# All eight heads in each recurrence step, and a written order for the conv's products between the steps

## The chip, the cores and the metric

The kernel runs on one core of a Trainium2 chip. The metric is the device time of one execution in microseconds (us); lower is better. An execution counts from its start to its end, and the span of the profile is the part of it that the profiler's records cover.

The engines are named as in the profile: PE is TensorE (matrix products), DVE is VectorE, ACT is ScalarE, POOL is GpSimd, SP is SyncE, which only issues transfers here. Each engine works through its own queue; engines wait for one another by semaphores.

## What is computed

The reference is a model of two layers over a sequence of T = 512 positions with D = 1024 channels, batch 1. Layer 0 mixes with a conv branch and an RWKV-7 branch, layer 1 with windowed attention; each is followed by a gated feed-forward block. The change touches layer 0's mixer, cut here to what matters:

```python
def conv_rwkv_mixer(x, ...):
    p = rms_norm(x, norm_g) @ w_in
    c = p[..., :2 * CONV_W] + conv_in_b                       # CONV_W = 512
    c = c[..., :CONV_W] * jax.nn.sigmoid(c[..., CONV_W:])     # the gated inputs ("glu")
    c = causal_dwconv(c, conv_dw_w, conv_dw_b)                # 31 taps, each channel by itself
    c = jax.nn.silu(layer_norm(c, conv_ln_g, conv_ln_b, CONV_LN_EPS))
    ...                                                       # r, decay, k, v, a, b of 8 heads of 64
    y = rwkv7_recurrence(rh, hs(decay), kh, vh, -kk, kk * hs(a))
    ...                                                       # group norm, bonus term, gate
    return jnp.concatenate([c, y], axis=-1) @ w_out

def step(s, inp):                                             # one position of the recurrence
    r_t, w_t, k_t, v_t, a_t, b_t = inp
    sa = jnp.einsum('bhij,bhj->bhi', s, a_t)
    s = s * w_t[:, :, None, :] + sa[..., None] * b_t[:, :, None, :] + v_t[..., None] * k_t[:, :, None, :]
    return s, jnp.einsum('bhij,bhj->bhi', s, r_t)
```

## The kernel before

Channels lie on the 128 partitions and positions along the free axis, so a tensor of 512 channels is four tiles of 128x512. Matrix products with a 1024-wide weight are made of three parts (high half by high half, and twice a high half by a low half): L150 casts a weight to its high half `whi` on ACT, L151 subtracts to get its low half `wlo` on DVE, and L174 is the product. L183 and L184 do the same to an activation.

**The recurrence** works in chunks of L = 64 positions: NCH = 8 chunks one after another, 8 heads in each. Ahead of it stands the inversion of small triangular systems; its last part are products of 32x32 tiles, L520 and L527, in two halves `g` of two groups of 32 products, whose results ACT copies to `tg` (L522) and `mbt` (L529). A chunk is worked in two half-steps `g` of four heads. Each half-step has five groups of products on TensorE:

- px, L543: operators times the stacked tile `sv` (rows 0 to 63 the state of the chunk, rows 64 to 127 the values), copied to `xs` (L545, on DVE for the first half, on ACT for the second);
- py, L549: the output's first part;
- pu, L556, which needs `xs`; ACT copies it over the old state (L558);
- pS, L562, the new state, which needs that copy. DVE puts it into `sv` of the next chunk: for chunk 0 as a copy (L566), later with the decayed old state `ds` (L553) added (L568);
- py's second part, L570; ACT copies py to `y` (L572).

The px of the next chunk reads the state that L566 or L568 wrote.

**The conv branch**: `glu(j)` makes one block of 128 channels of gated inputs (two products with the weight, L464 to L468, a sigmoid on ACT). Blocks 1 to 3 go through DRAM (`cpad`), come back shifted in four phases as `st` (loads L628, issued by POOL), and are convolved on TensorE, L633: 32 products per block, in groups of four that fill the four column strips, with the weights spread on diagonals `dg` (L623, DVE). L635 on ACT takes a finished block to `accs[j]`. Block 0 has its 31 taps on DVE: L618 on ACT starts the accumulator and 30 instructions of L620 add a tap each. `accs` of the four blocks go through a LayerNorm: sums over blocks L641 to L643, the split L183/L184, a product with ones L647, L652 takes the mean off, L653 squares, the same sums again (`lv`), a reciprocal root, L659 and a SiLU, and the split into `mc`. The group norm of the recurrence's output (L595 to L612) runs in two halves of the sequence and gives `mr`. The output projection takes all of `mc` first, then all of `mr`.

**What sets the order.** A scheduler (the Tile framework) orders the instructions of each engine from the code as written and from its own costs; it sets the conv's products between the recurrence's groups. In the code, the recurrence comes first, then the gated inputs, then the conv; a `table` call marks where ACT switches its function table, and work of that table is tied to it. `banks` and `psum` hand out TensorE's output banks in turn.

Of the kernel before, what the change touches and what calls it, by code (L numbers as in the profile page):

```python
# [19 lines left out]
P = 128  # L20
T = 512
# [7 lines left out]
CST = 540  # L29
# [39 lines left out]
class Net:  # L69
# [186 lines left out]
    def mixer(self):  # L256
# [7 lines left out]
        with ExitStack() as es:  # L264
# [234 lines left out]
            for fc in range(4):  # L499
                values(fc)  # L500

            zp = cst.tile([P, CK - 1], F32, name="zp")
            G.memset(zp, 0.0)
            for j in range(CC):
# [2 lines left out]
            m32 = cst.tile([P, 1, 1, 32], F32, name="m32")  # L507
            for s in range(4):
                G.tensor_copy(m32[s * 32 : s * 32 + 32, 0, 0, :], self.ident[s * 32 : s * 32 + 32, s * 32 : s * 32 + 32])
            mbu = mbt.rearrange("p f e c t -> p (f e c) t")  # L510
            svu = sv.rearrange("p f e c t -> p (f e c) t")
            for d in (1, 0):
# [18 lines left out]


            ys = [el([P, 2, 2, T // 2], "y") for _ in range(2)]
            half = lambda p0: self.psum()[p0 : p0 + 64, 0:256].rearrange("p (h i) -> p h i", h=4)
            heads = [(h, h // 2, h % 2) for h in range(4)]
            for c in range(NCH):
                for g in range(2):
                    mt = mts[g]
                    fs = slice(2 * g, 2 * g + 2)
                    st = sv[0:64, fs, :, c, :]  # L540
                    px = half(64)
                    for h, f, e in heads:
                        nc.tensor.matmul(px[:, h, :], lhsT=mt[:, f, e, c, 0:L], rhs=sv[:, 2 * g + f, e, c, :], start=True, stop=True)  # L543
                    xs = tr.tile([P, 4, L], F32, tag="xs", name="xs", bufs=2)[64:128]
                    (S.copy if g else V.tensor_copy)(xs, px)  # L545

                    py = self.psum()[:, 0 : 2 * L].rearrange("p (f t) -> p f t", f=2)
                    for h, f, e in heads:
                        nc.tensor.matmul(py[e * 64 : e * 64 + 64, f, :], lhsT=sv[:, 2 * g + f, e, c, :], rhs=mt[:, f, e, c, L:P],  # L549
                                         start=f == 0, stop=False)  # L550
                    if 0 < c < NCH - 1:
                        ds_ = tr.tile([64, 2, 2, L], F32, tag="xs", name="ds", bufs=2)
                        V.tensor_tensor(out=ds_, in0=st, in1=dl[:, fs, :, c : c + 1].to_broadcast([64, 2, 2, L]), op=ALU.mult)  # L553
                    pu = half(0)
                    for h, f, e in heads:
                        nc.tensor.matmul(pu[:, h, :], lhsT=mbt[64:128, 2 * g + f, e, c, :], rhs=xs[:, h, :], start=True, stop=True)  # L556

                    S.copy(st, pu.rearrange("p (f e) i -> p f e i", f=2))  # L558
                    if c < NCH - 1:
                        pS = half(0)  # L560
                        for h, f, e in heads:
                            nc.tensor.matmul(pS[:, h, :], lhsT=bkt[:, 2 * g + f, e, c, :], rhs=sv[:, 2 * g + f, e, c, :], start=True, stop=True)  # L562
                        pS4 = pS.rearrange("p (f e) i -> p f e i", f=2)
                        so = sv[0:64, fs, :, c + 1, :]
                        if c == 0:
                            V.tensor_copy(so, pS4)  # L566
                        else:
                            V.tensor_tensor(out=so, in0=pS4, in1=ds_, op=ALU.add)  # L568
                    for h, f, e in heads:
                        nc.tensor.matmul(py[e * 64 : e * 64 + 64, f, :], lhsT=sv[0:64, 2 * g + f, e, c, :],  # L570
                                         rhs=mbt[0:64, 2 * g + f, e, c, :], start=False, stop=f == 1)
                    S.copy(ys[g][:, 2 * c // NCH, :, c % 4 * L : (c % 4 + 1) * L], py)  # L572

            self.table("sigmoid_and_others")
            cp0 = ta("glu0")
            for j in range(CC):
                glu(j)
            self.table("natural_log_exp_and_others")


            g2 = ta("g2")
# [31 lines left out]
                    self.split(mr[:, 0, fs, ts], mr[:, 1, fs, ts], y)  # L613


            lt = self.act.tile([P, 2, CC, T], F32, tag="xgl", name="lt")
            accs, sqs = [[lt[:, o, j, :] for j in range(CC)] for o in range(2)]
# [3 lines left out]
            for j in range(1, CC):  # L621
                dg = tr.tile([P, 4, 8, 32], F32, tag="ep", name="dg", bufs=2)
                V.tensor_tensor(out=dg, in0=self.pcs("conv_dw", P)[:, 32 * j : 32 * j + 32].rearrange("p (q g o) -> p q g o", q=4, o=1).to_broadcast([P, 4, 8, 32]), in1=m32.to_broadcast([P, 4, 8, 32]), op=ALU.mult)  # L623
                stk = []
                for q in (2 * j, 2 * j + 1):
                    st = tr.tile([P, 2, CST], F32, tag="t4", name="st", bufs=T4)
                    for s in range(4):
                        G.dma_start(st[s * 32 : s * 32 + 32], cpad[q * 64 : q * 64 + 64, s : s + CST].rearrange("(b p) t -> p b t", p=32))  # L628
                    stk += [st[:, 0], st[:, 1]]
                pc = self.pmm()  # L630
                for g in range(8):
                    for b in range(4):
                        nc.tensor.matmul(pc[b * 32 : b * 32 + 32, :], lhsT=dg[:, b, g, :], rhs=stk[b][:, 4 * g : 4 * g + T],  # L633
                                         start=g == 0, stop=g == 7, tile_position=(0, b * 32))
                S.activation(out=accs[j], in_=pc, func=AF.Identity, bias=self.pc("conv_dw_b", j))  # L635


            def total(zs, name):
# [406 lines left out]
```

## Time and profile before

| | us |
|---|---|
| device time, median of three runs | 1218.25 |
| lowest and highest of the three | 1217.0 and 1220.24 |
| the profiled execution, its own time | 1216.95 |
| span of its profile | 1215.2 |
| PE busy in the span | 1194.8 (98%) |
| DVE busy | 723.4 (60%) |
| ACT busy | 554.3 (46%) |
| POOL busy | 72.0 (6%) |
| mean granted clock of PE | 0.996 |

The share of busy time is a mean over a kernel whose stages differ: the two feed-forward blocks are long rows of products, layer 0's mixer a dependent chain of small ones. A shape such as `128*64 128x64` in a row is what a product reads of its weights and what it streams; an fp32 product has two records in the trace. The time before an instruction stands in brackets with what ended it.

### The profile page before, as it was taken

How to read it: one execution, taken by the hardware profiler on the slowest of the kernel's cores; microseconds unless marked ns; L12 is line 12 of the kernel's file. 1: busy time of each engine (PE TensorE's matmuls, PEld its weight loads, DVE VectorE, ACT ScalarE, POOL GpSimd, SP SyncE). 2: the span in 40 equal slices, each digit the busy share in tenths (PEclk: the TensorE clock that was granted, in tenths of full speed). 3: DMA queues.
4: the chain of work that ended last, by engine and by line, in shares of the span. 5: the costliest groups of instructions: out<-in, count | busy, mean ns of one | idle time of the engine just before them, and what ended most of it. 6: DMA issues, size and time to landing. Idle time of an engine off the chain costs nothing.

```text
span 1215.2 us, 16956 instructions
## 1 busy us (share of the span) xinstructions
PE 1194.8 (98%) x6419; PEld 940.5 (77%) x6419; DVE 723.4 (60%) x1366; ACT 554.3 (46%) x1035; POOL 72.0 (6%) x209
## 2 busy tenths in 40 slices
PE   6999999999999999999999999999999999999998
PEld 5777866568788888888888866668888888888886
DVE  6787866477766555553333778875555555553332
ACT  6878332374534444342222567764543343442221
POOL 4101031000100000000000031100000000000000
PEclk9999998999999999999999999999999999999999
DMA  6144291023322223233333231112222223233331
GB/s 191 37 130 113 96 221 38 2 88 103 97 92 104 94 97 104 87 104 96 96 96 95 87 95 57 41 36 90 101 90 101 103 89 104 88 103 112 113 113 61
DMA packets 65088, 114.43 MB, mean 94 GB/s; under 512 B 15680, under 2 KB 17936, under 8 KB 65008
## 3 DMA queue, kind: packets, MB, share of 16 engines
q1 hardware_dynamic: 60048, 102.25, 26.3%
q0 software_dynamic: 4816, 10.89, 3.5%
q8 instruction: 50, 0.82, 0.3%
q14 instruction: 30, 0.25, 0.1%
q10 hardware_dynamic: 144, 0.23, 0.1%
HBM read 105.40 MB, written 4.26 MB: 90 GB/s over the span
## 4 chain that ended last, share of the span: by engine, by line
PE 94%; DVE 2%; ACT 2%; DMA 1%; issue 1%; SPq 0%; DVEq 0%
PE mm L174 68%; PE bank L174 11%; PE mm L633 2%; PE bank L931 2%; PE bank L957 1%; PE bank L950 1%; PE ps L411 1%; PE ps L543 1%; DMA xT<-in_xT_dram 1%; PE ps L562 1%; PE ps L556 1%; PE ps L570 0%; PE bank L359 0%; PE ps L549 0%; PE ps L520 0%
## 5 line engine op out<-in xcount | busy, mean ns | idle before, releaser
L151 DVE TENSOR_TENSOR wlo<-wraw,whi 128x512 fp32r<-128x512 f32 x364 | 250.8, 690 | 348.0 <-ACT whi L150 347.4
L150 ACT CAST whi<-wraw 128x512 fp32r<-128x512 f32 x364 | 224.9, 619 | 421.3 <-PE mm L174 378.4
L174 PE MATMUL mm<-xgh,whi 128*128 128x512 f32 x896 | 350.9, 392 | 9.8 <-ACT whi L150 8.3
L174 PE MATMUL mm<-xgh,wlo 128*128 128x512 f32 x896 | 351.0, 392 | 0.2 <-DVE wlo L151 0.2
L174 PE MATMUL mm<-xgl,whi 128*128 128x512 f32 x896 | 350.5, 391 | 0.0
L174 PEld LDWEIGHTS mm<-xgh,whi 128*128 128x128 f32 x896 | 168.6, 188 | 47.0 <-ACT whi L150 10.1
L174 PEld LDWEIGHTS mm<-xgh,wlo 128*128 128x128 f32 x896 | 168.5, 188 | 38.7 <-issue 2.4
L174 PEld LDWEIGHTS mm<-xgl,whi 128*128 128x128 f32 x896 | 168.7, 188 | 35.8 <-issue 1.2
L174 PE MATMUL mm<-hh,whi 128*128 128x512 f32 x352 | 136.9, 389 | 0.0
L174 PE MATMUL mm<-hl,whi 128*128 128x512 f32 x352 | 136.9, 389 | 0.0
L174 PE MATMUL mm<-hh,wlo 128*128 128x512 f32 x352 | 136.9, 389 | 0.0
L174 PEld LDWEIGHTS mm<-hh,wlo 128*128 128x128 f32 x352 | 66.1, 188 | 13.8
L174 PEld LDWEIGHTS mm<-hh,whi 128*128 128x128 f32 x352 | 66.1, 188 | 13.8
L174 PEld LDWEIGHTS mm<-hl,whi 128*128 128x128 f32 x352 | 66.1, 188 | 13.5
L720 DVE SCALAR_TENSOR_TENSOR t<-gp,col,t 128x512 f32<-128x512 f32 x88 | 63.5, 745 | 0.0
L717 ACT ACTIVATE t<-gp,col 128x512 f32<-128x512 f32 x44 | 35.7, 816 | 35.3 <-DVE gp L715 34.7
L183 ACT CAST hh<-t 128x512 fp32r<-128x512 f32 x44 | 27.2, 622 | 36.8 <-DVE t L723 36.5
L715 DVE TENSOR_TENSOR gp<-mm,rstd 128x512 f32<-128x512 f32 x44 | 30.3, 692 | 17.3 <-PE mm L174 17.2
L723 DVE TENSOR_TENSOR t<-t,mm 128x512 f32<-128x512 f32 x44 | 30.1, 687 | 17.0 <-PE mm L174 17.0
L101 ACT ACTIVATE t<-t 128x512 f32<-128x512 f32 x44 | 27.7, 630 | 20.4 <-DVE t L720 20.3
L714 POOL MEMSET gp<- 128x2 f32 x44 | 4.5, 104 | 507.7 <-DVE t L720 451.0
L936 DVE CUSTOM_DVE_ANT_0 pr<-bank,mask,nsnk 128x256 f32<-128x256 f32 (+1 forms) x64 | 31.4, 503 | 1.9 <-PE bank L931 1.9
(328 smaller groups left out, 1433.6 us busy)
## 6 DMA issues: line engine op xcount, KB each, us to landing
wraw<-in_w_up_dram SPq DMA_DIRECT2D x88, 512.0 KB, 3.5
wraw<-in_w_down_dram SPq DMA_DIRECT2D x40, 512.0 KB, 3.5
wraw<-in_w_in_dram SPq DMA_DIRECT2D x22, 512.0 KB, 3.6
wraw<-in_w_qkv_dram SPq DMA_DIRECT2D x12, 512.0 KB, 3.5
wraw<-in_w_out_dram SPq DMA_DIRECT2D x8, 512.0 KB, 3.5
wraw<-in_w_o_dram SPq DMA_DIRECT2D x8, 512.0 KB, 3.5
st<-cpad POOLq DMA_DIRECT2D x24, 135.0 KB, 4.4
xT<-in_xT_dram SPq DMA_DIRECT2D x4, 512.0 KB, 8.2
```

Source lines behind the costliest of these rows:

```text
L101: ins = self.nc.scalar.activation(**kw)
L150: nc.scalar.copy(hi, src)
L151: nc.vector.tensor_tensor(out=lo, in0=src, in1=hi.bitcast(F32), op=ALU.subtract)
L174: mm = lambda a, b, **kw: self.nc.tensor.matmul(ps, lhsT=a[:, i, k, :], rhs=b[:, kk, :], **kw)
L183: nc.scalar.copy(hi, src)
L633: nc.tensor.matmul(pc[b * 32 : b * 32 + 32, :], lhsT=dg[:, b, g, :], rhs=stk[b][:, 4 * g : 4 * g + T], start=g == 0, stop=g == 7, tile_pos ...
L715: V.tensor_tensor(out=gp[:, 2:], in0=pg[i], in1=rstd, op=ALU.mult)
L717: S.activation(out=t, in_=gp[:, 2:], func=AF.Identity, scale=self.pc("ffn_conv_w", (3 * l + 2) * FC + f), bias=self.pc("ffn_conv_b", l * F ...
L720: V.scalar_tensor_tensor(out=t, in0=gp[:, j : j + T], scalar=self.pc("ffn_conv_w", (3 * l + j) * FC + f), in1=t, op0=ALU.mult, op1=ALU.add)
L723: V.tensor_tensor(out=t, in0=t, in1=pu[i], op=ALU.mult)
L931: nc.tensor.matmul(pscs[e][:, hp, :nk], lhsT=qr[hs, h // 2, bs], rhs=kd[m][hs, k0 : k0 + nk], start=True, stop=True)
L936: V.tensor_tensor_reduce(out=pr_[:, i, :nk], in0=pscs[e][:, hp, :nk], in1=mask[:, 2 * P - nk :], op0=ALU.add, op1=ALU.min, scale=rq[:, b, ...
```

## The change

1. **Gated inputs.** The loop over `glu(j)` with its table switches moves from behind the recurrence to ahead of the triangles' products, in the order 1, 2, 3, 0.
2. **Conv products in a written order.** The loads, `dg` and the products of a block are issued by a generator, `conv_steps`, four products at a time. `cover(8)` sets the 32 products of block 1 ahead of the triangles' products; then each chunk calls it behind py, behind pu, and for chunks 0 to 3 behind py's second part. The generator is used up with the second burst of chunk 5. Within `tc.manual_schedule(engines={nc.tensor.engine})`, chunks 0 to 5 keep TensorE's instructions in the order of the code. The orders of DVE, ACT and POOL stay the scheduler's.
3. **Eight heads in a step.** Each chunk is one step; groups are of eight products, and copies are 512 wide. `xs` is copied by ACT alone. py takes one whole bank of ring "n".

Line numbers move: L543 px is L587 in the kernel after, L545 is L589, L549 L593, L553 L598, L556 L601, L558 L603, L562 L608, L566 and L568 L612 and L614, L570 L616, L572 L620; L520 is L566, L522 L568, L527 L573, L529 L575; L620 is L666, L623 L524, L633 L539, L635 L542, L641 to L643 L672 to L674, L595 L643, L600 L648, L609 L657, L647 L678, L652 L683.

```diff
@@ ahead of the triangles' products
+            self.table("sigmoid_and_others")
+            cp0 = ta("glu0")
+
+            for j in (1, 2, 3, 0):
+                glu(j)
+            self.table("natural_log_exp_and_others")
...
+            def conv_steps():
+                for j in range(1, CC):
+                    dg, stk = cv[j]
+                    pc = self.pmm()
+                    for g in range(8):
+                        for b in range(4):
+                            nc.tensor.matmul(pc[b * 32 : b * 32 + 32, :], lhsT=dg[:, b, g, :], rhs=stk[b][:, 4 * g : 4 * g + T],
+                                             start=g == 0, stop=g == 7, tile_position=(0, b * 32))
+                        if g == 7:
+                            S.activation(out=accs[j], in_=pc, func=AF.Identity, bias=self.pc("conv_dw_b", j))
+                            if j + 2 < CC:
+                                conv_load(j + 2)
+                        yield
+
+            conv_load(1)
+            conv_load(2)
+            steps = conv_steps()
+
+            def cover(n):
+                for _ in range(n):
+                    next(steps, None)
+
+            cover(8)
@@ the recurrence
-            heads = [(h, h // 2, h % 2) for h in range(4)]
-            for c in range(NCH):
+            heads = [(h, h // 2, h % 2) for h in range(8)]
+            eight = lambda p0: self.psum()[p0 : p0 + 64].rearrange("p (h i) -> p h i", h=8)
+
+            def chunk(c, cover):
...
+                px = eight(64)
+                for h, f, e in heads:
+                    nc.tensor.matmul(px[:, h, :], lhsT=mts[f // 2][:, f % 2, e, c, 0:L], rhs=sv[:, f, e, c, :], start=True, stop=True)
+                xs = td_("xs")[64:128].rearrange("p (h i) -> p h i", h=8)
+                S.copy(xs, px)
+
+                py = self.bank("n")[:, 0 : 4 * L].rearrange("p (f t) -> p f t", f=4)
...
+                cover(1)
+                if 0 < c < NCH - 1:
+                    ds_ = tb_("ds")[0:64].rearrange("p (f e i) -> p f e i", f=4, e=2)
+                    V.tensor_tensor(out=ds_, in0=st, in1=dl[:, :, :, c : c + 1].to_broadcast([64, 4, 2, L]), op=ALU.mult)
+                pu = eight(0)
...
+                S.copy(st, pu.rearrange("p (f e) i -> p f e i", f=4))
+                cover(1)
+                if c < NCH - 1:
+                    pS = eight(0)
...
+                    so = sv[0:64, :, :, c + 1, :]
+                    if c == 0:
+                        V.tensor_copy(so, pS4)
+                    else:
+                        V.tensor_tensor(out=so, in0=pS4, in1=ds_, op=ALU.add)
...
+                cover(c < 4)
                 for g in range(2):
...
+                    S.copy(ys[g][:, 2 * c // NCH, :, c % 4 * L : (c % 4 + 1) * L], py[:, 2 * g : 2 * g + 2, :])
+
+            with tc.manual_schedule(engines={nc.tensor.engine}):
+                for c in range(NCH - 2):
+                    chunk(c, cover)
+            for c in range(NCH - 2, NCH):
+                chunk(c, cover)
```

What this does to the order of the instructions is shown at three places.

TensorE in the kernel before, from the last weight products of the gated inputs through the triangles to the first half-steps (`st,dg` are the conv's products, `tg,sv` and `mbt,tg` the triangles', `sv,mt` px, `mt,sv` py, `xs,mbt` pu, `sv,bkt` pS):

```order
L633 MATMUL mm<-st,dg 32x512 x29
L520 MATMUL ps<-tg,sv 32x32 x32
L633 MATMUL mm<-st,dg 32x512 x4
L527 MATMUL ps<-mbt,tg 32x32 x32
L633 MATMUL mm<-st,dg 32x512
L520 MATMUL ps<-tg,sv 32x32 x32
L527 MATMUL ps<-mbt,tg 32x32 x32
L543 MATMUL ps<-sv,mt 64x64 x4
L549 MATMUL ps<-mt,sv 64x64 x4
L556 MATMUL ps<-xs,mbt 64x64 x4
L633 MATMUL mm<-st,dg 32x512 x3
L562 MATMUL ps<-sv,bkt 64x64 x4
```

The same place on TensorE in the kernel after, through step 0:

```order
L539 MATMUL mm<-st,dg 32x512 x32
L566 MATMUL ps<-tg,sv 32x32 x32
L573 MATMUL ps<-mbt,tg 32x32 x32
L566 MATMUL ps<-tg,sv 32x32 x32
L573 MATMUL ps<-mbt,tg 32x32 x32
L587 MATMUL ps<-sv,mt 64x64 x8
L593 MATMUL bank<-mt,sv 64x64 x8
L539 MATMUL mm<-st,dg 32x512 x4
L601 MATMUL ps<-xs,mbt 64x64 x8
L539 MATMUL mm<-st,dg 32x512 x4
L608 MATMUL ps<-sv,bkt 64x64 x8
L616 MATMUL bank<-mbt,sv 64x64 x8
```

The triangles' four groups now stand in one run behind all of block 1's conv products, and each group of a step has eight products.

DVE in the kernel before, around the first copy of a state, the L566 of chunk 0's first half (`lt` is the accumulator of conv block 0, `glu_1916` its gated input):

```order
L151 TENSOR_TENSOR wlo<-wraw,whi 128x512
L545 COPY xs<-ps 64x256
L620 SCALAR_TENSOR_TENSOR lt<-glu_1916,col,lt 128x498
L620 SCALAR_TENSOR_TENSOR lt<-glu_1916,col,lt 128x497
L620 SCALAR_TENSOR_TENSOR lt<-glu_1916,col,lt 128x496
L566 COPY sv<-ps 64x4x64
L620 SCALAR_TENSOR_TENSOR lt<-glu_1916,col,lt 128x495
```

DVE in the kernel after, where 11 of the 30 accumulates, `dg` and L151 stand ahead of the twelfth:

```order
L524 TENSOR_TENSOR dg<-col,m_1590 128x1024
L666 SCALAR_TENSOR_TENSOR lt<-glu_1272,col,lt 128x505
L666 SCALAR_TENSOR_TENSOR lt<-glu_1272,col,lt 128x504
L666 SCALAR_TENSOR_TENSOR lt<-glu_1272,col,lt 128x503
L666 SCALAR_TENSOR_TENSOR lt<-glu_1272,col,lt 128x502
L666 SCALAR_TENSOR_TENSOR lt<-glu_1272,col,lt 128x501
L151 TENSOR_TENSOR wlo<-wraw,whi 128x512
L666 SCALAR_TENSOR_TENSOR lt<-glu_1272,col,lt 128x500
```

Seventeen more L666 follow without a break, and then on the same engine:

```order
L666 SCALAR_TENSOR_TENSOR lt<-glu_1272,col,lt 128x482
L672 TENSOR_TENSOR lm<-lt 128x512
L612 COPY sv<-ps 64x8x64
L598 TENSOR_TENSOR ds<-sv,dl 64x512
L614 TENSOR_TENSOR sv<-ps,ds 64x8x64
```

The first copy of a state, L566 before and L612 after, moved from between the accumulates to behind the last of them and behind the first sum of the LayerNorm.

DVE in the kernel before, around the later sums of the LayerNorm (`lm`); the L568 behind them are state sums of later half-steps:

```order
L553 TENSOR_TENSOR ds<-sv,dl 64x256
L642 TENSOR_TENSOR lm<-lt 128x512
L596 TENSOR_TENSOR y<-y,bank 128x512
L643 TENSOR_TENSOR lm<-lm 128x512
L596 TENSOR_TENSOR y<-y,bank 128x512
L568 TENSOR_TENSOR sv<-ps,ds 64x4x64
```

DVE in the kernel after, at the same sums; the L614 ahead of them is the last state sum, of step 6:

```order
L598 TENSOR_TENSOR ds<-sv,dl 64x512
L614 TENSOR_TENSOR sv<-ps,ds 64x8x64
L673 TENSOR_TENSOR lm<-lt 128x512
L674 TENSOR_TENSOR lm<-lm 128x512
L644 TENSOR_TENSOR y<-y,bank 128x512
L184 TENSOR_TENSOR lmh<-lm,lmh 128x512
```

The second and third sums moved behind the last state sum of the recurrence.

## Rows read from the trace of the kernel before

**Rows 1.** The page's first part: engine, busy us, share, instructions.

```profile
PE 1194.8 (98%) x6419; PEld 940.5 (77%) x6419; DVE 723.4 (60%) x1366; ACT 554.3 (46%) x1035; POOL 72.0 (6%) x209
```

**Rows 2.** Windows view: stretch, length, each engine's busy us, clock, DMA share, GB/s.

```profile
170.79:307.79 137.00, 134.22 (x1301) 91.40 (x1300) 92.93 (x160) 64.97 (x123) 9.10 (x18) 0.98 0.24 70
```

**Rows 3.** Waits of PE, 170 to 309: us in total, times, longest.

```profile
PE ps L562 <- ACT sv L558: 1.1, 2, 0.6
```

**Rows 4.** Timeline of PE, conv burst and triangles: start, us, engine, instruction, count.

```profile
170.79 7.05 PE L633 MATMUL mm<-st,dg 128*32 128x512 f32 x58
177.78 2.21 PE L520 MATMUL ps<-tg,sv 32*32 32x32 f32 x64
179.91 1.06 PE L633 MATMUL mm<-st,dg 128*32 128x512 f32 x8
```

**Rows 5.** Timeline of PE, a steady half-step, and a later px.

```profile
213.86 0.68 PE L543 MATMUL ps<-sv,mt 128*64 128x64 f32 x8
214.47 1.06 PE L633 MATMUL mm<-st,dg 128*32 128x512 f32 x8
215.47 0.45 PE L549 MATMUL ps<-mt,sv 128*64 128x64 f32 x8
215.85 0.68 PE L556 MATMUL ps<-xs,mbt 64*64 64x64 f32 x8
216.46 1.07 PE L633 MATMUL mm<-st,dg 128*32 128x512 f32 x8
...
238.43 0.62 PE L543 MATMUL ps<-sv,mt 128*64 128x64 f32 x7
```

**Rows 6.** Windows view, behind the triangles and at the kernel's end.

```profile
188.10:195.10 7.00, 6.81 (x56) 4.64 (x54) 4.69 (x8) 1.51 (x4) 2.52 (x5) 0.51 0.59 144
...
1212.00:1213.00 1.00, 0.00 (x0) 0.00 (x0) 0.00 (x0) 0.00 (x0) 0.00 (x0) 0.63 0.34 131
```

**Rows 7.** Timeline of PE at the kernel's start.

```profile
7.65 0.80 PE L174 MATMUL mm<-xgh,whi 128*128 128x512 f32 x1 [7.65 <-ACT whi L150]
...
10.86 0.39 PE L174 MATMUL mm<-xgl,whi 128*128 128x512 f32 x1
```

**Rows 8.** Timeline of DVE, accumulates, dg, a weight's low half, first state copy.

```profile
173.42 6.21 DVE L620 SCALAR_TENSOR_TENSOR lt<-glu,col,lt 128x510 f32<-128x510 f32 x8
181.03 1.23 DVE L623 TENSOR_TENSOR dg<-col,m 128x1024 f32<-128x1024 f32 x1 [1.39 <-PE mm L633]
...
188.43 0.69 DVE L151 TENSOR_TENSOR wlo<-wraw,whi 128x512 fp32r<-128x512 f32 x1 [3.20 <-ACT whi L150]
...
189.61 2.28 DVE L620 SCALAR_TENSOR_TENSOR lt<-glu,col,lt 128x498 f32<-128x498 f32 x3
193.70 0.42 DVE L566 COPY sv<-ps 64x256 f32<-64x256 f32 x1 [1.81 <-PE ps L562]
```

**Rows 9.** Timeline of ACT, the last sigmoid, the table, a triangle copy, a cast.

```profile
171.69 0.72 ACT L101 ACTIVATE sg<-sg,col 128x512 f32<-128x512 f32 x1 [0.20 <-DVE sg L464]
172.43 1.28 ACT L91 ACT_TABLE_LOAD   x1
...
187.18 0.58 ACT L529 COPY mbt<-ps 32x512 f32<-32x512 f32 x1 [0.33 <-PE ps L527]
187.78 0.62 ACT L150 CAST whi<-wraw 128x512 fp32r<-128x512 f32 x1
```

**Rows 10.** Timelines of ACT, DVE and PE, conv's end to the first cast of mc.

```profile
229.31 0.69 ACT L635 ACTIVATE lt<-mm,col 128x512 f32<-128x512 f32 x1 [1.34 <-PE mm L633]
230.03 0.69 DVE L642 TENSOR_TENSOR lm<-lt 128x512 f32<-128x512 f32 x1 [0.78 <-ACT lt L635]
...
257.70 0.62 ACT L183 CAST mc<-cact 128x512 fp32r<-128x512 f32 x1
257.85 1.12 PE L595 MATMUL bank<-y,bdm 128*128 128x512 f32 x2 [0.22 <-ACT y L572]
```

**Rows 11.** Timeline of POOL, loads of st.

```profile
186.36 4.26 POOL L628 DMA_DIRECT2D st<-cpad  x8
```

More of the change, by code (lines that the diff above doesn't have):

```diff
@@ L509, in mixer, with conv_load @@
                 G.tensor_copy(m32[s * 32 : s * 32 + 32, 0, 0, :], self.ident[s * 32 : s * 32 + 32, s * 32 : s * 32 + 32])
+            lt = self.act.tile([P, 2, CC, T], F32, tag="xgl", name="lt")
+            accs, sqs = [[lt[:, o, j, :] for j in range(CC)] for o in range(2)]
+            cv = {}
+            def conv_load(j):
+                dg = tr.tile([P, 4, 8, 32], F32, tag="ep", name="dg", bufs=2)
+                V.tensor_tensor(out=dg, in0=self.pcs("conv_dw", P)[:, 32 * j : 32 * j + 32].rearrange("p (q g o) -> p q g o", q=4, o=1).to_broadcast([P, 4, 8, 32]), in1=m32.to_broadcast([P, 4, 8, 32]), op=ALU.mult)
+                stk = []
+                for q in (2 * j, 2 * j + 1):
+                    st = tr.tile([P, 2, CST], F32, tag="t4", name="st", bufs=T4)
+                    for s in range(4):
+                        G.dma_start(st[s * 32 : s * 32 + 32], cpad[q * 64 : q * 64 + 64, s : s + CST].rearrange("(b p) t -> p b t", p=32))
+                    stk += [st[:, 0], st[:, 1]]
+                cv[j] = dg, stk
+            def conv_steps():
[18 more added lines that the diff above has]
+            cover(8)
             mbu = mbt.rearrange("p f e c t -> p (f e c) t")
@@ L533, in mixer @@
             ys = [el([P, 2, 2, T // 2], "y") for _ in range(2)]
-            half = lambda p0: self.psum()[p0 : p0 + 64, 0:256].rearrange("p (h i) -> p h i", h=4)
-            heads = [(h, h // 2, h % 2) for h in range(4)]
-            for c in range(NCH):
-                for g in range(2):
[L538 to L578, printed above, removed]
+            heads = [(h, h // 2, h % 2) for h in range(8)]
+            eight = lambda p0: self.psum()[p0 : p0 + 64].rearrange("p (h i) -> p h i", h=8)
+            def chunk(c, cover):
+                st = sv[0:64, :, :, c, :]
+                px = eight(64)
[4 more added lines that the diff above has]
+                py = self.bank("n")[:, 0 : 4 * L].rearrange("p (f t) -> p f t", f=4)
+                for h, f, e in heads:
+                    nc.tensor.matmul(py[e * 64 : e * 64 + 64, f, :], lhsT=sv[:, f, e, c, :], rhs=mts[f // 2][:, f % 2, e, c, L:P],
+                                     start=f == 0, stop=False)
+                cover(1)
[3 more added lines that the diff above has]
+                pu = eight(0)
+                for h, f, e in heads:
+                    nc.tensor.matmul(pu[:, h, :], lhsT=mbt[64:128, f, e, c, :], rhs=xs[:, h, :], start=True, stop=True)
+                S.copy(st, pu.rearrange("p (f e) i -> p f e i", f=4))
+                cover(1)
+                if c < NCH - 1:
+                    pS = eight(0)
+                    for h, f, e in heads:
+                        nc.tensor.matmul(pS[:, h, :], lhsT=bkt[:, f, e, c, :], rhs=sv[:, f, e, c, :], start=True, stop=True)
+                    pS4 = pS.rearrange("p (f e) i -> p f e i", f=4)
+                    so = sv[0:64, :, :, c + 1, :]
[3 more added lines that the diff above has]
+                        V.tensor_tensor(out=so, in0=pS4, in1=ds_, op=ALU.add)
+                for h, f, e in heads:
+                    nc.tensor.matmul(py[e * 64 : e * 64 + 64, f, :], lhsT=sv[0:64, f, e, c, :],
+                                     rhs=mbt[0:64, f, e, c, :], start=False, stop=f == 3)
+                cover(c < 4)
+                for g in range(2):
+                    S.copy(ys[g][:, 2 * c // NCH, :, c % 4 * L : (c % 4 + 1) * L], py[:, 2 * g : 2 * g + 2, :])
```

17 lines of the change are left out of this document (removed).

## The prediction

> **What bounds the kernel now.** I read the page's first part first: TensorE is busy 98% of the span [rows 1], so time goes where TensorE waits, or where its own work is slow. The change touches only layer 0's mixer, from the conv's first product at 170.79 us to the end of the output projection at 307.79 us: 137.0 us, of which TensorE is busy 134.2 and idle 2.8 [rows 2]. The view of waits says what ends that idle time: the largest entry is the state copy, 0.55 us at each of two places [rows 3]. No large wait is there to be removed.
>
> The timeline of TensorE then gives the price of each kind of work. The opening conv burst, 29 products of two records each, takes 7.0 us; a group of 32 triangle products takes 2.13 us, start to start [rows 4]. In a steady half-step of four heads, px and pu cost 0.61 us a group, py 0.38, and four conv products 1.0 [rows 5]; pS is taken like px, and py's second half like py.
>
> Last, the windows with the granted clock. From 188.1 to 195.1, right after the triangles' groups, TensorE runs at 0.51 of its clock, which is the lower level, 1.2 GHz: 7 us, of which half of the busy 6.8, 3.4, is lost. After the kernel's last product TensorE stands idle, and its clock falls to a mean of 0.63 in 1212 to 1213 [rows 6]. At the start it takes from 7.65 to 10.86 for a product to shrink from 0.80 to 0.39 us [rows 7].
>
> **The change part by part.**
>
> *Eight heads in a step.* The products stay the same; their runs of one shape become half as many. Seven records of a px group take 0.62 us, eight 0.68 [rows 5]: 0.06 each, so of a group's 0.61 some 0.13 is fixed. Doubled without it, px, pu and pS are 1.07, py and py's second half 0.62. Counted over the recurrence, changes of shape on TensorE fall from some 91 to 47: 44 x 0.13 = 5.7 us saved. If py pays no fixed part (its 0.38 can be read either way), 16 fewer count and 3.6 is saved. I take 5.7, since the 0.38 is below eight records of 0.06. The old idle 2.8 goes too.
>
> A step with three bursts of four conv products is 1.07 + 0.62 + 1.0 + 1.07 + 1.0 + 1.07 + 0.62 + 1.0 = 7.45 us. ACT's and DVE's copies double in width, to some 0.6 and 0.7 us (a 512-wide copy is 0.58 [rows 9], a 512-wide subtraction 0.69 [rows 8]); a burst of 1.0 covers each. Uncovered are the state's sum (0.7, with 0.15 for hand-overs, an estimate, behind a py of 0.62) at the three step changes from 4 to 7, 0.23 each, and the state copy of step 6, 0.73: together 1.4 us. With half the width that copy held TensorE for 0.55 [rows 3], the nearest row.
>
> *The DVE queue at the first step change.* This is the step that decides. The 30 accumulates of conv block 0 were spread between the copies; in the program of after they all stand on DVE ahead of the copy of the state from chunk 0 to 1, and with them a dg, a weight's low half (L151) and the first sum of the LayerNorm (L672). TensorE's px of step 1 reads that state.
>
> TensorE first: 32 conv products at 0.24 us, 170.79 + 7.7 = 178.5; four triangle groups, 187.0; step 0, 7.45: it is done at 194.45. Now DVE: the last sigmoid ends at 172.4, the table load at 173.7, the start of the accumulator (an ACTIVATE, 0.72 like the sigmoid) at 174.4 [rows 9]. Six accumulates at 0.77 [rows 8]: 179.1. dg, 1.23: 180.3. Five more: 184.2. Here L151 waits for the cast whi, which stands on ACT behind the third copy of the triangles: 3.5 groups after 178.5 is 186.0, then a copy of 0.58 and a cast of 0.62 [rows 9] with hand-over, 187.3. L151: 188.0. Nineteen accumulates at 0.76: 202.4. L672 at 0.65 and the copy at 0.65: 203.7. **TensorE waits from 194.45 to 203.65: 9.2 us.** Behind px on TensorE's queue stands everything else, conv products too, so nothing fills the hole. In before the same copy, of half the width, started at 193.70, ahead of the later accumulates [rows 8].
>
> *The tail.* Steps 1 to 3 end at 203.65 + 22.35 = 226.0; step 4 (6.45 and a wait) at 232.7; the conv ends in step 5 at 237.4 instead of 229.3 [rows 10]; step 6's state is there at 244.7. On DVE the next two sums of the LayerNorm stand behind that state's sum, so the chain can only go on at 244.7. From there to the end of the first cast of mc took 28.3 us in before, 230.03 to 258.32 [rows 10], with half-steps in between. Fourteen DVE operations and nine of ACT at 0.65, a table load of 1.28 and 1.0 of TensorE's sums are 17.3 in a straight line. I take the middle, 22.8, because the group norm's operations still stand between the links while the steps are nearly gone: mc at 267.5. TensorE has until then step 7 without pS, 3.4 from 244.8, and the norms' products (three L643 and two L648 at 1.06, start to start, as L595 [rows 10]; four L657 and four L678, taken at half of it), 9.5: its work would end at 257.7. **The tail costs 9.8 us**, between 4.3 and 15.3. In before it cost nothing.
>
> *The clock.* The fall at 188 comes again, since the triangles now stand in one run. Before it cost 3.4; now it lies ahead of a hole that DVE ends, so there it costs only what it delays the cast that L151 waits for, 0 to 1.7 (0.9). The hole is an idle time as after the last product: TensorE comes out of it at half clock, at least for the 3.2 us that the start shows, some 1.4 lost, at most for before's fall, 3.4 (2.4 is the middle). The tail's waits cost 0 to 3.4 (2.0). Together 5.3, between 1.4 and 8.5.
>
> The trace shows the fall after a wait only where the kernel ends. The Trainium skill, "TensorE: Matmul & The Clock Gate", section "HAM oscillation — how this bites in real kernels", tells of kernels whose every wait between bursts brings the half clock back, and which pay for it each time. By it the hole and the tail both pay, as forecast; a kernel of this shape against which the rule does not hold would come to near 1227.
>
> *Moved loads and glu.* The gated inputs are the same four pairs of products in another order: nothing. The memset of sv now stands on POOL behind eight loads of st, 4.26 us in before [rows 11]: 178.5 + 4.3 = 182.8, ahead of step 0 at 187.0, so hidden; a load that came 4 us late would only eat into the hole. SP's queue is as it was.
>
> *The sum.* 137.0 - 2.8 - 3.4 (clock) = 130.8; - 5.7 + 9.2 + 1.4 + 9.8 = 145.5; + 5.3 = 150.8. That is +13.8 on the profiled run's 1216.95: 1230.75. The median of the three runs lies 1.3 above the profiled run: **1232**. The low end, tail 4.3 and clock 1.4: 130.8 - 5.7 + 9.2 + 1.4 + 4.3 + 1.4 = 141.4, +4.4, 1222.7. The high end, 3.6 saved, tail 15.3, clock 8.5: 161.6, +24.6, 1242.9.
>
> **The rivals.**
>
> 1. *The waits come, the clock costs nothing more*: 145.5, +8.5, 1227. For it: before's fall came after narrow products, not after a wait. Against: the fall after the last product.
>
> 2. *The tail at its worst*: the chain is as slow as in before, 5.5 more than forecast, 1237. For it: the group norm's operations stand between its links. Against: most half-steps are gone.
>
> 3. *The other side, faster*: DVE reaches the state copy by 194.4, because the accumulates run at half their price once no other copies break them up. Then the 9.2 and its clock are gone: 130.8 - 5.7 + 1.4 + 4.3 = 130.8, -6.2, 1212; with the middle tail and its clock 138.3, 1219. It decides if the 30 accumulates, dg and L151 take less than 20 us from 174.4 on. Against: eight in a row took 6.21 [rows 8].
>
> 4. *It doesn't do what it says*: half as many runs of one shape save nothing, because the 0.13 belongs to the records and not to the group. Then 5.7 is missing: 1238. For it: the fixed part rests on one pair of rows.
>
> The Trainium skill, same page, section "Architectural detail: the array is 16× 32×32, not 1× 128×128", says that VectorE's queue is strict first-in first-out. The DVE rows of before stand in the program's order, which agrees; a queue that let the copy pass would bring rival 3.
>
> **How the numbers follow.** The forecast has 0.62, rival 1 0.13, rival 2 0.11, rival 4 0.08, rival 3 0.06. The range 1221 to 1241 leaves out rival 3 and the ends of 2 and 4. About 0.3% (3.7 us) is what a measurement of this kernel can tell from no change. Faster by more: 0.04, the lower half of rival 3; within: 0.05, the rest of it and the low end of the forecast; slower: 0.91.
>
> **What would show it.** In the trace of after: one wait of TensorE of 6 to 10 us before px (L587), ended by the copy L612; DVE's accumulates in one run up to it; a half clock before and after it; steps 1 to 3 of 7.45 us each; 4 to 15 us of waits ahead of the first mc product. It is wrong if the copy L612 comes out ahead of most accumulates, if a step of three bursts takes 8.2 (two half-steps of 4.6 less a burst), or if the LayerNorm's chain is hidden behind steps 6 and 7.

## The result

The kernel after takes 1225.71 us, the median of four runs (1224.53 to 1228.36), against 1217.86 (1217.0 to 1220.24) for the kernel before: 1.0064 times as long, with a 95% interval from 1.0046 to 1.0082. It is slower, by 7.9 us; forecast were 1232 and a range of 1221 to 1241. The profiled run of after is the slowest of its four, 1228.36, span 1226.7, so its trace shows 11.5 us more than that of before.

**Where the time went.** The windows view of after shows the stage of [rows 2], from the conv's first product to the end of the output projection, and its stretches at the lower clock:

```profile
171.02:317.77 146.75, 132.04 (x1301) 93.03 (x1300) 88.58 (x138) 65.22 (x115) 5.83 (x12) 0.90 0.20 60
...
183.00:193.50 10.50, 10.50 (x150) 8.65 (x148) 7.00 (x10) 3.51 (x6) 0.52 (x1) 0.52 0.13 30
204.00:208.00 4.00, 3.91 (x42) 2.95 (x43) 0.72 (x2) 0.58 (x1) 0.00 (x0) 0.65 0.01 4
257.50:272.00 14.50, 11.54 (x22) 6.58 (x23) 13.97 (x26) 9.97 (x16) 0.00 (x0) 0.53 0.00 1
```

The stage is 146.75 us instead of 137.0, and TensorE is idle for 14.7 of them instead of 2.8. It is at half clock in three places instead of one [rows 6]: through the triangles and step 0, in step 1, and from the tail into the output projection. The second fall begins inside the hole (0.99 from 199 to 200 us, 0.50 from 200 on). The view of waits of TensorE (165 to 320) says what ends the idle time; in before its largest entry was [rows 3]:

```profile
PE ps L587 <- DVE sv L612: 6.4, 1, 6.4
PE mm L678 <- ACT lvh L183: 4.0, 1, 4.0
PE bank L643 <- DVE gn L652: 2.1, 1, 2.1
...
PE ps L608 <- ACT sv L603: 0.7, 1, 0.7
PE bank L657 <- DVE y L660: 0.6, 1, 0.6
PE ps L587 <- DVE sv L614: 0.5, 3, 0.2
```

The first line is the hole ahead of step 1. The next two and the L657 are the tail, 6.9 us with a last 0.2: 4.2 of it is ended by the LayerNorm's chain (`lvh`), 2.7 by the group norm's (`gn` and `y`). DVE's timeline shows what stood ahead of the copy L612; its accumulates are those of [rows 8]:

```profile
174.80 4.66 DVE L666 SCALAR_TENSOR_TENSOR lt<-glu,col,lt 128x511 f32<-128x511 f32 x6 [1.38 <-ACT lt L664]
179.38 1.22 DVE L524 TENSOR_TENSOR dg<-col,m 128x1024 f32<-128x1024 f32 x1
180.52 3.85 DVE L666 SCALAR_TENSOR_TENSOR lt<-glu,col,lt 128x505 f32<-128x505 f32 x5
187.61 0.69 DVE L151 TENSOR_TENSOR wlo<-wraw,whi 128x512 fp32r<-128x512 f32 x1 [3.25 <-ACT whi L150]
188.22 14.50 DVE L666 SCALAR_TENSOR_TENSOR lt<-glu,col,lt 128x500 f32<-128x500 f32 x19
202.75 0.69 DVE L672 TENSOR_TENSOR lm<-lt 128x512 f32<-128x512 f32 x1
203.36 0.68 DVE L612 COPY sv<-ps 64x512 f32<-64x512 f32 x1
```

DVE is busy all the way from 187.61 to 204; the copy is last in a row of work, most of which could come later, as e1 shows. TensorE's timeline has the hole, and then a steady step, whose groups answer to [rows 5]:

```profile
204.09 1.65 PE L587 MATMUL ps<-sv,mt 128*64 128x64 f32 x13 [6.44 <-DVE sv L612]
...
212.59 0.97 PE L587 MATMUL ps<-sv,mt 128*64 128x64 f32 x13
...
214.13 1.06 PE L539 MATMUL mm<-st,dg 128*32 128x512 f32 x8
215.13 1.14 PE L601 MATMUL ps<-xs,mbt 64*64 64x64 f32 x16
...
219.88 0.97 PE L587 MATMUL ps<-sv,mt 128*64 128x64 f32 x13
...
266.66 3.08 PE L174 MATMUL bank<-mc,whi 128*128 128x512 f32 x5
```

Step 1, at half clock at first, takes 8.5 us (204.09 to 212.59), step 2 takes 7.29. The first product with mc starts at 266.66; in before it started at 259.29. The LayerNorm's chain that leads to it goes on with the second sum on DVE, right behind the state's sum of step 6, and ends with the casts of mc on ACT:

```profile
245.69 0.67 DVE L673 TENSOR_TENSOR lm<-lt 128x512 f32<-128x512 f32 x1
```

```profile
266.00 1.12 ACT L183 CAST mc<-cact 128x512 fp32r<-128x512 f32 x2
```

### The profile page after: what moved, and what is told of

The parts are those of the page before. It is cut to its first block, busy times and chain, and to the rows that moved or that the text cites. A ratio compares the mean times of both kernels' runs of the same rounds, so it can differ in the third digit from the quotient of the medians.

```text
span 1226.7 us, 16917 instructions
## 1 busy us (share of the span) xinstructions
PE 1194.7 (97%) x6419; PEld 943.5 (77%) x6419; DVE 719.4 (59%) x1345; ACT 554.6 (45%) x1027; POOL 72.0 (6%) x209
## 4 chain that ended last, share of the span: by engine, by line
PE 92%; DVE 4%; ACT 2%; DMA 1%; issue 1%; SPq 0%; DVEq 0%; ACTq 0%
PE mm L174 67%; PE bank L174 11%; PE bank L962 2%; PE mm L539 2%; PE bank L988 1%; PE bank L981 1%; DVE lt L666 1%; PE ps L411 1%; DMA xT<-in_xT_dram 1%; PE ps L601 1%; PE ps L587 1%; PE ps L608 1%; PE bank L359 0%; PE bank L643 0%; DVE wlo L151 0%
## 5 line engine op out<-in xcount | busy, mean ns | idle before, releaser
L151 DVE TENSOR_TENSOR wlo<-wraw,whi 128x512 fp32r<-128x512 f32 x364 | 250.6, 690 | 345.1 <-ACT whi L150 344.5
L174 PEld LDWEIGHTS mm<-hl,whi 128*128 128x128 f32 x352 | 66.1, 188 | 13.8
L174 PEld LDWEIGHTS mm<-hh,wlo 128*128 128x128 f32 x352 | 66.1, 188 | 13.8
L748 ACT ACTIVATE t<-gp,col 128x512 f32<-128x512 f32 x44 | 35.7, 816 | 35.3 <-DVE gp L746 34.7
L746 DVE TENSOR_TENSOR gp<-mm,rstd 128x512 f32<-128x512 f32 x44 | 30.3, 692 | 17.3 <-PE mm L174 17.2
```

Source lines behind the costliest of these rows:

```text
L151: nc.vector.tensor_tensor(out=lo, in0=src, in1=hi.bitcast(F32), op=ALU.subtract)
L174: mm = lambda a, b, **kw: self.nc.tensor.matmul(ps, lhsT=a[:, i, k, :], rhs=b[:, kk, :], **kw)
L746: V.tensor_tensor(out=gp[:, 2:], in0=pg[i], in1=rstd, op=ALU.mult)
L748: S.activation(out=t, in_=gp[:, 2:], func=AF.Identity, scale=self.pc("ffn_conv_w", (3 * l + 2) * FC + f), bias=self.pc("ffn_conv_b", l * F ...
```

## The experiments

Ten kernels were run. e1 and e5 are edits of the kernel after, e4 of the kernel before, e2 and e3 of e1; e6 to e10 go on from e3. Each diff shows what is added. Times are medians; the ratio is to runs of the kernel before on the same chip.

### e1: the state copy first

```diff
-                        V.tensor_copy(so, pS4)
+                        self.first = V.tensor_copy(so, pS4)
...
-                V.scalar_tensor_tensor(out=accs[0][:, k:], ...)
+                ins = V.scalar_tensor_tensor(out=accs[0][:, k:], ...)
+                if k == 16:
+                    self.after(ins, self.first)
```

> The kernel after with one order added on VectorE: the 16th accumulate of conv block 0 and all behind it come after the first copy of a state. Nothing else changes. My theory (the hole is VectorE's queue): the 6.4 us wait of TensorE ahead of step 1 goes, and with it the 1.3 us that step 1 loses at half clock; the triangles and step 0 still run at half clock, and the tail stays with some 7 us of waits. Some 7.7 us less than after, 1217 to 1219. Rival (the accumulates are a fixed load that something later waits for): the sums of the LayerNorm come later by what the copy gained, the wait moves to the tail, and the time stays at 1224 to 1227.

Measured: 1218.87 (1216.94 to 1220.14) beside 1217.18, ratio 1.001 (1.000 to 1.002). One order between two instructions of DVE takes the time from 1225.71 to 1218.87, 6.8 us less. The wait ahead of step 1 is gone, and step 1 begins at full clock, straight behind step 0, with no idle time in its row:

```profile
196.83 0.97 PE L587 MATMUL ps<-sv,mt 128*64 128x64 f32 x13
```

The rival falls: nothing later waits longer, the tail's waits are as in after, 6.9 us in all.

```profile
PE mm L680 <- ACT lvh L183: 3.9, 1, 3.9
PE bank L643 <- DVE gn L652: 1.8, 1, 1.8
```

So the hole was DVE's queue, and without it the kernel is within 0.2% of before. What the eight heads save goes, by this trace, to the tail's waits and to more time at half clock; no run takes these two apart.

### e2: conv products between the triangles'

On e1: `cover(8)` ahead of the triangles becomes `cover(0)`, their loops go under the written order, and

```diff
                     S.copy(tg[96:128, u0 : u0 + 16, :], pg[96:128])
+                    cover(1)
...
                     S.copy(mbu[64:96, gu, LH:L], pg[64:96])
+                    cover(1)
```

> As e1_copy_first, and the eight groups of four conv products that stood ahead of the triangles' products stand between them, one behind every 16; the steps keep their groups. My theory (it is the run of narrow products that lowers the clock): the clock stays up through triangles and step 0, some 4.9 us come back, and eight more breaks of shape cost some 1.7: 3 us less than e1_copy_first, 1214 to 1216. Rival (a fall comes whatever stands between): 1 to 2 us more than e1_copy_first.

Measured: 1235.54 (1233.65 to 1236.28), ratio 1.0146 (1.0125 to 1.0166). Both forecasts are wrong: it is 16.7 us slower than e1, not 3 faster and not 2 slower. The timeline of TensorE and the windows show two things that I had not counted:

```profile
174.10 1.89 PE L567 MATMUL ps<-tg,sv 32*32 32x32 f32 x32 [3.42 <-DMA tg<-tnd]
```

```profile
173.00:174.00 1.00, 0.00 (x0) 0.00 (x0) 0.02 (x1) 0.99 (x2) 0.00 (x0) 0.54 0.91 109
174.00:206.00 32.00, 31.90 (x349) 18.11 (x350) 12.99 (x17) 6.54 (x12) 2.42 (x5) 0.50 0.11 37
```

With the conv's burst gone from ahead of the triangles, their first product waits 3.4 us for a load that the burst had covered. The clock falls in that wait (0.54 in its last us) and then stays at half for 32 us, through the mixture of triangle and conv products and into step 0: some 16 us lost where e1 loses 5 (11.9 us at 0.57). The wait of 3.4 and the clock's 11 are 14.4 of the 16.7. The 1.7 expected for the breaks would bring it to 16.1; it was not measured by itself.

### e3: the LayerNorm's chain sooner

On e1: `cover(12)` instead of `cover(8)`, so that the conv ends in step 3, and the code in another order:

```diff
             with tc.manual_schedule(engines={nc.tensor.engine}):
-                for c in range(NCH - 2):
+                for c in range(4):
                     chunk(c, cover)
-            for c in range(NCH - 2, NCH):
-                chunk(c, cover)
+            ...                                # accumulates of block 0, sums lm, mean, squares
+            chunk(4, cover)
+            chunk(5, cover)
+            rs = self.rsqrt_rows(tr, "tb", total(sqs, "lv"), 1e-5, "ln", ln=True)
+            chunk(6, cover)
+            chunk(7, cover)
...
-            group_norm(0)
             self.table("silu_and_others")
...
             self.table("natural_log_exp_and_others")
+            group_norm(0)
             group_norm(1)
```

> As e1_copy_first, with the tail changed: 12 groups of conv products ahead of the triangles so that the conv ends in step 3, the LayerNorm's sums written ahead of chunks 4 and 6, and the first half of the group norm behind the SiLU. My theory (the tail waits because the LayerNorm's chain starts when step 6 is over): the first product with mc comes when the steps end; 7 us of waits and up to 4 us of half clock behind them go, and some 4 us of small waits of the uncovered steps 4 to 7 come: 6 to 7 us less than e1_copy_first, 1210 to 1213. Rival (VectorE and ScalarE are full there, so mc comes at the same time): no change against e1_copy_first, 1217 to 1219.

Measured: 1214.52 (1212.14 to 1217.31), ratio 0.9975 (0.9962 to 0.9987). It is 4.4 us less than e1, not the 6 to 7 expected, and faster than before. Of the tail's 6.9 us of waits 1.0 is left; new ones stand in steps 4 to 7:

```profile
PE ps L608 <- ACT sv L603: 2.9, 3, 2.1
PE ps L587 <- DVE sv L614: 2.1, 2, 1.7
```

The rival (DVE and ACT full) falls, since mc comes when the steps end. The 2.1 and the 1.7 are copies of the recurrence behind the LayerNorm's work on ACT and DVE: the pattern of the hole in small. Behind the 2.1 the clock falls again, from 242 to 245. e3 moves the end of the conv, the sums and the first half of the group norm together; which of them took the tail's waits away was not tried.

### e4: eight heads and nothing else

The kernel before with the eight-head step in place of the two half-steps, without the moved gated inputs and without a written order.

> The kernel before with eight heads in a step and nothing else: gated inputs behind the recurrence, no written order. My theory: the fixed part of the groups is saved, but in this program the scheduler sets the whole recurrence ahead of the gated inputs and the conv, so nothing stands between the steps: about 1.2 us of waits in each of 8 steps, and behind the conv the norms' chains stand alone with 15 to 25 us of waits: 1240 to 1255. Rival (eight heads are worth their 5.7 us by themselves): 1212 to 1214.

Measured: 1252.85 in one run, in the expected range, but not by the expected sum:

```profile
PE ps L520 <- DMA tg<-tnd: 13.8, 1, 13.8
PE ps L560 <- ACT sv L556: 4.7, 7, 0.7
PE mm L649 <- ACT lvh L183: 4.1, 1, 4.1
PE bank L602 <- DVE gn L606: 3.0, 1, 3.0
```

The scheduler now sets the triangles ahead of the gated inputs as well, and their first product waits 13.8 us for the same load as in e2. The steps' waits are 7.2 us (4.7 and two smaller lines, 1.5 for xs and 1.0 for the state's sum), the norms' 12.4. The half clock, which the expectation left out, costs some 18 more (22.9 us busy at 0.51 from 152 to 187 us, 13.9 at 0.53 from 274 to 296). So the eight-head step alone loses 35.7 us in this run. Only the 7.2 are its own uncovered copies; the rest comes with the order that the scheduler then chooses, and the other two parts of the change are what makes the step usable.

### e5: the hole filled

The kernel after, with this behind the last `cover` of chunk 0:

```diff
+                if c == 0:
+                    fill = self.psum("fill")
+                    for _ in range(5):
+                        nc.tensor.matmul(fill, lhsT=self.bdm, rhs=cp0, start=True, stop=True)
```

> The kernel after with five products of 128x512 in fp32 set on TensorE behind step 0 (1.06 us each, 5.3 us; they are written to a bank that nobody reads, the rest is as in after), so that the 6.4 us hole ahead of step 1 is filled to within some 1.1 us. Theory (it is the idle hole that brings the half clock of step 1): the hole still ends at 204 by VectorE's copy, the clock stays up, and step 1 takes 7.3 us instead of 8.5: 1.2 to 1.6 us less, 1223 to 1226. Rival (the half clock of step 1 is left over from the triangles, or comes from step 1 itself): step 1 takes 8.5 again, no change.

Measured: 1225.41 in one run. The time decides nothing; the windows do:

```profile
200.10:202.29 2.19, 0.02 (x2) 0.00 (x1) 2.08 (x5) 0.00 (x0) 0.00 (x0) 1.00 0.00 0
202.29:203.80 1.51, 1.51 (x32) 1.48 (x32) 1.26 (x2) 0.33 (x1) 0.00 (x0) 0.97 0.00 0
203.80:210.50 6.70, 6.70 (x43) 3.18 (x42) 0.00 (x0) 0.83 (x2) 0.00 (x0) 0.50 0.01 2
```

A wait of 2.2 us stayed, because the products took 4.6 us instead of 5.3. The clock was up through that wait, and it fell 1.5 us after TensorE had gone on with px and py. So my theory as I put it, that the idle hole is all that counts, is not borne out; nor is the rival, since e1 has the same step 1 without a wait, at full clock. Step 1 took 10.35 us here (202.29 to 212.64), longer than the 8.50 of after, although the hole was two thirds filled. What comes behind a wait counts too. In after itself the clock had fallen inside the hole, at 200 us.

### e6 to e10: holding the clock

These go on from e3. e6 sets four conv groups ahead of the triangles, one behind every 16 triangle products (the `cover(1)` of e2), so the load has come when the first triangle wants it. e7 sets four ahead, six between the triangles' halves, two behind:

```diff
-            cover(12)
+            cover(4)
...
+                cover((6, 2)[g])
```

> As e3_early_chain, with four of the 12 early groups of conv products ahead of the triangles and one behind every 16 triangle products, which takes away the wait on the load of tg that stood ahead of the triangles in e2_between. Theory now (in e2_between the wait of 3.4 us on that load lowered the clock, and the mixture of narrow and conv products did not raise it again): without the wait the clock is up when the mixture starts. If the mixture can hold the clock, the 3.9 us at half clock of e3_early_chain go and 1.7 of more breaks come: 1211 to 1213. Rival (the mixture lowers the clock by itself): it stays at half through 15 us of mixture, 6 to 8 us more than e3_early_chain, 1219 to 1223.

> As e3_early_chain, with its 12 early groups of conv products set as four ahead of the triangles' first half, six between the halves and two behind the second, so that the triangles stand in two runs of 4.3 us instead of one of 8.5. In after and in e3_early_chain the clock fell some 5.3 us after the run began. Theory: neither run is long enough, the clock stays up, and some 3.9 us of half clock go for 0.3 of breaks: 1210 to 1212. Rival (two runs six us apart count together): the clock falls in the second run or behind it, 1213 to 1217 as e3_early_chain.

Measured: e6 1211.56 (1211.33 to 1211.83), ratio 0.995 (0.9935 to 0.9965); e7 1214.54 (1212.11 to 1219.36), ratio 0.9975 (0.9961 to 0.9989). The windows over the triangles, of e6 and then of e7:

```profile
174.70:191.60 16.90, 16.90 (x324) 9.92 (x320) 12.71 (x17) 6.10 (x11) 4.79 (x9) 1.00 0.38 107
```

```profile
183.83:187.00 3.17, 3.17 (x107) 3.17 (x104) 3.17 (x5) 1.17 (x3) 3.17 (x7) 1.00 0.93 247
187.00:193.50 6.50, 6.50 (x62) 3.46 (x60) 0.78 (x2) 1.14 (x2) 0.26 (x1) 0.50 0.22 49
```

The same mixture that stayed at half clock in e2 stays at full clock in e6, through 16.9 us: in these two runs it kept the level at which it started. e6's theory holds and its rival falls. e7's theory falls: the clock came down in the second run of triangles, in spite of 5.3 us of conv products between the runs. e6 is 3.0 us faster than e3. Its four runs lie within 0.5 us of each other, the ten of e3 and of e7 within 5 and 7; the profiled runs of e3 and e6 are only 0.8 us apart (1212.14, the fastest of e3's ten, and 1211.33), so most of the 3.0 lies in runs of e3 that left no trace.

e8 has `cover(6)` ahead instead of `cover(4)`; e9 has two groups behind every 32 triangle products instead of one behind every 16. e10 adds one order on ACT:

```diff
             self.table("silu_and_others")
+            self.after(self.set_load, self.st6)    # st6: the state copy of step 6
```

> As e6_between_covered, with six instead of four groups of conv products ahead of the triangles, so that the conv ends two groups sooner. In e6_between_covered TensorE waited 1.7 and 2.1 us in steps 4 to 6 for copies that stood behind the LayerNorm's work, and the clock was at half from 240 to 243.7 behind the second. Theory: the LayerNorm's operations fall clear of those copies, the longest wait is some 1 us, the clock does not fall, 2 to 3 us less: 1209 to 1211. Rival (the waits come at another place of the steps, since two more step bursts are uncovered): no change, 1211 to 1212.

> As e8_conv_sooner, with two groups of conv products behind every 32 triangle products instead of one behind every 16: half as many breaks. Theory: the mixture still holds the clock with runs of 2.1 us, and four fewer pairs of breaks give 0.5 to 1.1 us: 1208 to 1211. Rival (runs of 2.1 us are long enough to lower the clock, and once it is low the mixture keeps it there, as in e2_between): 3 to 8 us more than e8_conv_sooner.

> As e9_between_32, with one order more: ScalarE's load of the SiLU table comes after its state copy of step 6. In e9_between_32 that copy stood behind the table load (1.28 us), TensorE waited 2.06 us for it, and the clock was at half from 239 to 242.8. Theory (a wait of about 2 us among narrow products brings a fall, one of about 1 us does not): the wait shrinks to 0.8 to 1.0, the clock stays up, 1.1 + 1.5 to 2 us less: 1206 to 1208. Rival (the fall there comes from the narrow products of steps 5 to 7 without conv between): the wait shrinks and the fall stays, 1208 to 1209.

Measured: e8 1211.25 (1210.0 to 1211.53), ratio 0.9938 (0.9918 to 0.9958); e9 1209.67 (1208.8 to 1210.17), 0.9927 (0.9905 to 0.9949); e10 1206.63 (1206.51 to 1207.48), 0.9904 (0.9882 to 0.9927). In e8 the wait of 1.7 is gone and the 2.1 is not, the fall behind it stays, and waits for the state copies have grown from 2.9 to 4.1 us in all: 0.3 us less than e6, the rival's outcome. e9's runs of 2.1 us still hold the clock, and it is 1.6 us faster than e8, more than its breaks were expected to give. In the traces the breaks give 1.0, up to the end of the triangles; the rest is a shorter fall behind the 2.1 (3.85 us busy at 0.58, in e8 6.80 at 0.57). What was left is in the timelines of ACT, e9 first and e10 below:

```profile
235.02 1.28 ACT L91 ACT_TABLE_LOAD   x1
236.32 0.63 ACT L201 ACTIVATE ln_v<-ln_y 128x512 f32<-128x512 f32 x1
236.97 0.58 ACT L606 COPY sv<-ps 64x512 f32<-64x512 f32 x1
```

```profile
234.44 0.63 ACT L201 ACTIVATE ln_v<-ln_y 128x512 f32<-128x512 f32 x1
235.10 0.58 ACT L606 COPY sv<-ps 64x512 f32<-64x512 f32 x1
235.69 1.28 ACT L91 ACT_TABLE_LOAD   x1
```

With the table behind the copy, TensorE waits 0.8 instead of 2.06 us for it, and the fall behind it is gone too: in e9 the clock was at 0.58 from 239 to 243, in e10 the whole stage is at 1.00 (the windows of e9, then of e10):

```profile
239.00:243.00 4.00, 3.85 (x48) 3.35 (x43) 2.52 (x5) 1.63 (x4) 0.53 (x1) 0.58 0.00 0
```

```profile
170.50:297.46 126.96, 122.14 (x1301) 86.52 (x1300) 88.03 (x138) 65.22 (x115) 6.39 (x13) 1.00 0.23 68
```

So e10's theory holds and its rival falls. e10 beats before by 10.4 us and after by 19. Its stage is 127.0 us where before has 137.0 and after 146.8.

## Why the prediction came out as it did

**The hole: right, and to the step.** DVE began the accumulates at 174.8 (174.4 forecast), ended L151 at 188.3 (188.0), the last accumulate at 202.7 (202.4); TensorE went on at 204.09 (203.65). The wait is 6.4 us, not 9.2, because TensorE came to it at 197.65 instead of 194.45: the triangles and step 0 ran at half clock from 183 to 193. Since DVE sets the end, the forecast let that fall cost only what it delays the cast ahead of L151, 0 to 1.7. It delayed it by some 1.3, an estimate: ACT's copies of the triangles started 0.9 to 1.0 us apart up to 183.13, and 1.7 and 1.5 apart behind it. L151 was still within 0.3 of the forecast, because the first two groups of triangle products took 1.95 us each and not 2.13. e1 shows the cause: with the copy ahead, 6.8 us go.

**The saving of the eight heads: the mis-sized term.** I had 5.7 us, from 0.13 for each change of shape. Three conv bursts of 1.0 taken from the 7.29 of a step leave 4.29 for its groups; two half-steps of [rows 5] have 2 x (3 x 0.61 + 2 x 0.38) = 5.18. That is 0.89 per chunk, 7.1 in all; the prices that I had taken give 4.45 for a step's groups, 0.73 per chunk. The step of the working that failed is px with py: together they took 1.54 (212.59 to 214.13), not 1.07 + 0.62, so the fixed part that I had put between them does not show. In e10, where nothing falls, TensorE is busy 122.1 us in the stage; before, without its 3.4 of lost clock, 130.8: 8.7 saved, with the eight breaks of the triangles in it. Where the 1.6 beyond the 7.1 come from is not traced. Rival 4, no saving at all, falls: a step of three bursts took 7.29 us, not 8.2.

**The tail: right in place, wrong in its split.** The chain went on behind the state's sum of step 6, at 245.69 (244.7 forecast), and the first cast of mc began at 266.00; 20.9 us to its end, where I took 22.8 between 17.3 and 28.3. The idle time is 6.9, not 9.8, and the clock cost 5.4 (11.54 busy at 0.53), not 2.0: products at half clock fill the waits. Together they are 12.3, forecast 11.8. That the two errors nearly cancel is luck. The trace shows the chain's late start; that the late start made the waits is argued. In e3 they go when the chain starts sooner, but e3 also moves the first half of the group norm, which ended 2.7 of the 6.9.

**The clock.** Behind the hole 1.2 us were lost (8.50 for step 1, 7.29 for step 2), forecast 2.4, at the low end 1.4. Rival 1, no further cost, falls. The Trainium skill, "TensorE: Matmul & The Clock Gate", section "HAM oscillation — how this bites in real kernels", tells of a kernel in which the wait for a load behind each burst of products brings the half clock back, so that its cost is paid each time. For the hole (6.4 us) and the tail (4.0) the trace agrees. The waits of 2.06 us in e9 and of 1.7 us in e3 are shorter than those that the section tells of: behind the first the clock was at half, behind the second, at 228 to 232 us, at 1.00.

**The sum.** Forecast 150.8 for the stage, measured 146.75, which is 4.05 less. Along the path that sets the time the difference falls into four parts. To the end of the hole it took 33.07 us, forecast 33.76 with 0.9 for the fall: 0.7 less. From there to the chain's start it took 41.60, forecast 43.45 with 2.4 for the clock: 1.85 less, of which 1.2 is the clock. The chain took 1.9 less. From its end to the end of the stage it took 51.15, forecast 50.79 with the tail's 2.0 of clock: 0.4 more. So the saving beyond the forecast hardly shows in the time of after: most of it lies under the hole and under the tail's waits, whose ends TensorE does not set. Behind the stage the profiled run lost 1.5 more, to a fall that I had not thought of: in the attention, from 738 to 744, which before's profiled run does not have.

```profile
738.00:744.00 6.00, 6.00 (x26) 3.75 (x26) 5.36 (x23) 2.84 (x9) 1.50 (x3) 0.72 0.07 12
```

From there the median goes another way than I took it: I set it 1.3 above the profiled run, as in before; after's is 2.65 below, since it was the slowest of four. So 13.8 forecast on the profiled run is 11.4 there, and 7.9 between the medians: of the 6.3 us between 1232 and 1225.71, 3.95 is this choice of run and not the kernel.

**The rivals.** Rival 2, the tail at its worst, falls with 20.9 us for the chain. Rival 3, faster by way of DVE, needed the accumulates at half their price; nineteen in a row took 14.50, 0.76 each, as in [rows 8]. e10 shows that its direction was open all the same, with other orders of DVE, ACT and TensorE together.

## What to carry to other kernels

When the order of one engine is written by hand, the queues of the others decide when it waits: look in each of them for work without haste ahead of an instruction that the written chain needs, and tie that one ahead; here one such order, on DVE, was worth 6.8 us and another, on ACT, some 3. Merging steps saves the breaks between groups, but can take away the work that covered their copies and loads (7.2 and 13.8 us of waits in e4), so the cover is part of the change. Here narrow products were best mixed with wide ones from a start at full clock; a wait of 3.4 us ahead of them cost some 11 us more in e2.

## What the runs showed that was not expected

The same mixture of triangle and conv products ran at half clock for 32 us in e2, where a wait of 3.4 us stood ahead of it, and at full clock for 16.9 us in e6, where none did: in these two runs the level, once there, was kept. Why is open. In after, e1 and e3 the clock fell in the midst of one run of triangle products, which took 9.2 to 10.1 us with the fall; in e7 in the second of two runs of 4.1 and 4.6 us with 5.3 us of conv products between. In before, where single conv bursts stood between the first triangle groups, it fell behind a last run of 4.1 us (184.02 to 188.08). In all of these TensorE was busy up to the fall. In two of the twelve profiled runs, after's and e2's, the clock also falls in the attention near 740 us, in code that the change does not touch; what sets it off stays open. A wait of 2.2 us did not lower the clock while it lasted in e5, but 1.5 us later; how long and how narrow the work behind a wait must be was not tried.
